# Contrast adjustment: 64 KB rows in three kept buffers, two hardware queues, half-tile DMAs of every second row, and the clip shared between VectorE and ScalarE

## The chip, the cores and the metric

One core of one Trainium2 chip. The metric is device time in microseconds (us) of one execution. The profile adds a "span", from the first to the last instruction it shows, which is about 2 us (1.8 to 2.2 in the profiled runs) shorter than the device time of the same run. Every run of a kernel on one core is called fast unless it was over 1.5% above the fastest run of the same kernel. The first measurement and the three sets of experiments ran at different times, the three sets on three different chips; the kernel before ran beside every set.

## The reference

```python
x = rand(16, 3, 512, 512), float32          # 48 images of 1 MiB, 50.33 MB
mean = np.mean(x, axis=(2, 3), keepdims=True)
out = np.clip(mean + factor * (x - mean), 0, 1)     # factor 1.5
```

Nothing of an image can be written before all of it has been read, because its mean is needed first. So 100.66 MB cross the DMA engines, and each tile goes load, sum, clip, store.

## The kernel before

```python
TILE_IMGS = [4] * 11 + [2, 2]        # 4 MiB tiles of 32 KB rows, two small ones at the end
X_BUFS = 5
...
for i, N in enumerate(TILE_IMGS):
    xt = xpool.tile([P, NMAX * n_pix // P], f32, name="xt")[:, :FREE]
    nc.sync.dma_start(out=xt, in_=src)
    nc.vector.tensor_reduce(out=rsum, in_=xt, axis=X, op=add)          # L77
    nc.tensor.matmul(pbias, blockw[N], rsum, start=True, stop=True)    # L85
    nc.scalar.copy(out=bias, in_=pbias)
    nc.scalar.activation(out=xt, in_=xt, func=Relu, bias=bias, scale=factor)      # L90
    nc.vector.tensor_scalar(out=xt, in0=xt, scalar1=1.0, scalar2=None, op0=min)   # L97
    nc.gpsimd.dma_start(out=dst, in_=xt)                               # L104
```

(The rest sets up the constant matrix that sums over an image's partitions. Cuts are marked by dots.)

Of the kernel before, what the change touches and what calls it, by code (L numbers as in the profile page):

```python
# [1 line left out]

# [4 lines left out]


TILE_IMGS = [4] * 11 + [2, 2]  # L10
X_BUFS = 5
STORE_ENGINE = "gpsimd"


@with_exitstack
def kernel(
    ctx: ExitStack,
    tc: tile.TileContext,
    x: bass.AP,
    factor: float,  # L20
    out: bass.AP,
):
    nc = tc.nc
    P = 128

    B, C, H, W = x.shape
    n_img = B * C
    n_pix = H * W

    factor = float(factor)  # L30
    f32 = mybir.dt.float32

    assert sum(TILE_IMGS) == n_img
    NMAX = max(TILE_IMGS)

    x_f = x.rearrange("b c h w -> (b c h w)")
    out_f = out.rearrange("b c h w -> (b c h w)")

    wconst = (1.0 - factor) / float(n_pix)

    consts = ctx.enter_context(tc.tile_pool(name="consts", bufs=1))
    blockw = {}
    for N in sorted(set(TILE_IMGS)):
        wt = consts.tile([P, P], f32, name=f"blockw{N}")
        PPI = P // N
        if N == 1:
            nc.gpsimd.memset(wt, wconst)
        else:
            nc.gpsimd.memset(wt, 0.0)  # L49
            for b in range(N):  # L50
                nc.gpsimd.memset(wt[b * PPI : (b + 1) * PPI, b * PPI : (b + 1) * PPI], wconst)  # L51
        blockw[N] = wt

    xpool = ctx.enter_context(tc.tile_pool(name="xpool", bufs=X_BUFS))
    rpool = ctx.enter_context(tc.tile_pool(name="rpool", bufs=12))
    bpool = ctx.enter_context(tc.tile_pool(name="bpool", bufs=12))
    psum = ctx.enter_context(tc.tile_pool(name="psum", bufs=8, space=bass.MemoryType.PSUM))

    if STORE_ENGINE == "sync":
        store_eng = nc.sync  # L60
    elif STORE_ENGINE == "act":
        store_eng = nc.scalar
    else:
        store_eng = nc.gpsimd

    pix_off = 0
    for i, N in enumerate(TILE_IMGS):
        FREE = n_pix * N // P
        npix_tile = n_pix * N

        xt = xpool.tile([P, NMAX * n_pix // P], f32, name="xt")[:, :FREE]
        src = bass.AP(tensor=x_f.tensor, offset=pix_off, ap=[[FREE, P], [1, FREE]])
        dst = bass.AP(tensor=out_f.tensor, offset=pix_off, ap=[[FREE, P], [1, FREE]])
        nc.sync.dma_start(out=xt, in_=src)  # L74

        rsum = rpool.tile([P, 1], f32)
        nc.vector.tensor_reduce(  # L77
            out=rsum,
            in_=xt,
            axis=mybir.AxisListType.X,  # L80
            op=mybir.AluOpType.add,
        )

        pbias = psum.tile([P, 1], f32)
        nc.tensor.matmul(pbias, blockw[N], rsum, start=True, stop=True)  # L85

        bias = bpool.tile([P, 1], f32)
        nc.scalar.copy(out=bias, in_=pbias)  # L88

        nc.scalar.activation(  # L90
            out=xt,
            in_=xt,
            func=mybir.ActivationFunctionType.Relu,
            bias=bias,
            scale=factor,
        )
        nc.vector.tensor_scalar(  # L97
            out=xt,
            in0=xt,
            scalar1=1.0,  # L100
            scalar2=None,
            op0=mybir.AluOpType.min,
        )
        store_eng.dma_start(out=dst, in_=xt)  # L104

        pix_off += npix_tile


# [1 line left out]
_INS = ['x', 'factor']  # L110
_OUTS = [((16, 3, 512, 512), 'float32')]
#: Inputs that are plain numbers.
_NUMBERS = {'factor': 1.5}


# [26 lines left out]
```

## Time and profile before

| | kernel before |
|---|---|
| device time, median of 3 | 239.69 us (239.58 to 239.84) |
| span of the profiled run | 238.6 us |
| DMA over the span | 422 GB/s |
| VectorE, ScalarE busy | 66%, 37% |

The page of the kernel before, cut. The row DMA is the busy share of the 16 DMA engines, in tenths, in 40 slices of the span; q1 carries the loads, q0 the stores; the last three lines are groups of instructions with their busy time, the mean ns of one, and the idle time ahead of them with what ended it.

```profile
span 238.6 us, 238 instructions
...
DMA  7999999999999999999999999999999999999995
...
q1 hardware_dynamic: 1872, 50.33, 49.4%
q0 software_dynamic: 1872, 50.33, 49.0%
...
L77 DVE TENSOR_REDUCE rsum<-xt 128x1 f32<-128x8192 f32 (+1 forms) x13 | 104.4, 8029 | 61.7 <-DMA xt<-in_x_dram 61.7
L90 ACT ACTIVATE xt<-xt,bias 128x8192 f32<-128x8192 f32 (+1 forms) x13 | 85.8, 6598 | 0.4
L97 DVE TENSOR_SCALAR xt<-xt 128x8192 f32<-128x8192 f32 (+1 forms) x13 | 53.2, 4091 | 5.0 <-ACT xt L90 5.0
```

The DMA engines are busy throughout and VectorE waits 61.7 us for loads: the kernel is bound by DMA. The stretches view of the same trace gives the rate in the last column; the other columns are each engine's busy time.

```profile
core 0: us, PE busy (x) PEld busy (x) DVE busy (x) ACT busy (x) POOL busy (x), PEclk, DMA share, GB/s
60.00:180.00 120.00, 3.46 (x12) 3.00 (x12) 79.72 (x13) 48.97 (x13) 3.73 (x7) 1.00 1.01 435
210.00:230.00 20.00, 0.56 (x2) 0.50 (x2) 6.71 (x2) 3.87 (x2) 0.53 (x1) 1.00 1.00 432
```

The Trainium skill, "DMA: Bandwidth & Descriptors", section "Where 436 GB/s comes from", gives a ceiling of 435 GB/s; this trace sits on it. The same section says that the HBM side, at about 358 GB/s, binds for transfers between HBM and SBUF; this core ran at 435 GB/s, so that lower limit did not bind here. The timeline of the last small tile:

```profile
211.80 4.42 DVE L77 TENSOR_REDUCE rsum<-xt 128x1 f32<-128x4096 f32 x1 [4.14 <-DMA xt<-in_x_dram]
...
217.16 3.71 ACT L90 ACTIVATE xt<-xt,bias 128x4096 f32<-128x4096 f32 x1
220.90 2.29 DVE L97 TENSOR_SCALAR xt<-xt 128x4096 f32<-128x4096 f32 x1 [4.68 <-ACT xt L90]
223.49 0.53 POOL L104 DMA_DIRECT2D out_dram<-xt  x1 [15.00 <-DVE xt L97]
```

From the last landing (211.80) to the last store's issue (223.49) are 11.7 us.

### The profile page before, as it was taken

How to read it: one execution, taken by the hardware profiler on the slowest of the kernel's cores; microseconds unless marked ns; L12 is line 12 of the kernel's file. 1: busy time of each engine (PE TensorE's matmuls, PEld its weight loads, DVE VectorE, ACT ScalarE, POOL GpSimd, SP SyncE). 2: the span in 40 equal slices, each digit the busy share in tenths (PEclk: the TensorE clock that was granted, in tenths of full speed). 3: DMA queues.
4: the chain of work that ended last, by engine and by line, in shares of the span. 5: the costliest groups of instructions: out<-in, count | busy, mean ns of one | idle time of the engine just before them, and what ended most of it. 6: DMA issues, size and time to landing. Idle time of an engine off the chain costs nothing.

```text
span 238.6 us, 238 instructions
## 1 busy us (share of the span) xinstructions
PE 7.4 (3%) x26; PEld 6.5 (3%) x26; DVE 156.5 (66%) x26; ACT 89.1 (37%) x27; POOL 10.3 (4%) x25
## 2 busy tenths in 40 slices
PE   0000000000000000000000000000000000000000
PEld 0000000000000000000000000000000000000000
DVE  0088999999599079459629909917945979742300
ACT  2002966472906601900920650470190095406000
POOL 2000001000000000000000000000000000500000
DMA  7999999999999999999999999999999999999995
GB/s 269 434 439 439 439 439 352 439 434 439 439 439 439 439 434 434 423 428 412 423 439 439 434 439 439 439 439 439 434 428 426 426 404 428 431 434 439 428 434 214
DMA packets 3744, 100.66 MB, mean 422 GB/s; under 512 B 416, under 2 KB 416, under 8 KB 416
## 3 DMA queue, kind: packets, MB, share of 16 engines
q1 hardware_dynamic: 1872, 50.33, 49.4%
q0 software_dynamic: 1872, 50.33, 49.0%
HBM read 50.33 MB, written 50.33 MB: 422 GB/s over the span
## 4 chain that ended last, share of the span: by engine, by line
issue 38%; DMA 35%; DVE 18%; POOL 2%; POOLq 0%; SPq 0%
DMA xt<-in_x_dram 19%; DMA out_dram<-xt 16%; DVE rsum L77 11%; DVE xt L97 7%; POOL out_dram L104 2%; POOLq L137 0%; SPq L74 0%; POOLq L104 0%
## 5 line engine op out<-in xcount | busy, mean ns | idle before, releaser
L77 DVE TENSOR_REDUCE rsum<-xt 128x1 f32<-128x8192 f32 (+1 forms) x13 | 104.4, 8029 | 61.7 <-DMA xt<-in_x_dram 61.7
L90 ACT ACTIVATE xt<-xt,bias 128x8192 f32<-128x8192 f32 (+1 forms) x13 | 85.8, 6598 | 0.4
L97 DVE TENSOR_SCALAR xt<-xt 128x8192 f32<-128x8192 f32 (+1 forms) x13 | 53.2, 4091 | 5.0 <-ACT xt L90 5.0
L88 ACT COPY bias<-pbias 128x1 f32<-128x1 f32 x13 | 2.1, 160 | 130.6 <-PE pbias L85 130.6
L104 POOL DMA_DIRECT2D out_dram<-xt x13 | 9.0, 692 | 213.0 <-DVE xt L97 212.8
L85 PE MATMUL pbias<-rsum,blockw 128*128 128x1 f32 x26 | 7.4, 355 | 209.5 <-DVE rsum L77 209.5
L85 PEld LDWEIGHTS pbias<-rsum,blockw 128*128 128x128 f32 x26 | 6.5, 311 | 210.3 <-DVE rsum L77 107.1
L88 ACT ACT_TABLE_LOAD x1 | 1.3, 1283 | 0.8 <-PEq L123 0.8
L51 POOL MEMSET blockw<- 32x32 f32 (+1 forms) x6 | 0.8, 128 | 0.2
L49 POOL MEMSET blockw<- 128x128 f32 x2 | 0.3, 205 | 0.3 <-POOLq L123 0.3
L123 POOL MEMSET const-float32-0.0<- 128x1 f32 x1 | 0.1, 104 | 0.2 <-issue 0.2
L123 POOL MEMSET const-bfloat16-1.0<- 128x1 bf16 x1 | 0.1, 113 | 0.0
L123 POOL MEMSET const-uint8-127<- 128x1 uint8 x1 | 0.1, 113 | 0.0
L123 POOL MEMSET const-float32-1.0<- 128x1 f32 x1 | 0.1, 110 | 0.0
## 6 DMA issues: line engine op xcount, KB each, us to landing
xt<-in_x_dram SPq DMA_DIRECT2D x11, 4096.0 KB, 24.6
out_dram<-xt POOLq DMA_DIRECT2D x11, 4096.0 KB, 36.0
xt<-in_x_dram SPq DMA_DIRECT2D x2, 2048.0 KB, 19.5
out_dram<-xt POOLq DMA_DIRECT2D x2, 2048.0 KB, 19.1
```

What stands on the lines that cost most here:

```text
L49: nc.gpsimd.memset(wt, 0.0)
L51: nc.gpsimd.memset(wt[b * PPI : (b + 1) * PPI, b * PPI : (b + 1) * PPI], wconst)
L77: nc.vector.tensor_reduce(out=rsum, in_=xt, axis=mybir.AxisListType.X, op=mybir.AluOpType.add,)
L85: nc.tensor.matmul(pbias, blockw[N], rsum, start=True, stop=True)
L88: nc.scalar.copy(out=bias, in_=pbias)
L90: nc.scalar.activation(out=xt, in_=xt, func=mybir.ActivationFunctionType.Relu, bias=bias, scale=factor,)
L97: nc.vector.tensor_scalar(out=xt, in0=xt, scalar1=1.0, scalar2=None, op0=mybir.AluOpType.min,)
L104: store_eng.dma_start(out=dst, in_=xt)
L123: nc = _bacc.Bacc("TRN2", target_bir_lowering=False, num_devices=1)
```

## The change

The intent is to use larger descriptors, to feed both queues by hardware, and to share the compute so that 8 MB tiles (six of them) still fit under the DMA time. The core of the diff:

```diff
-TILE_IMGS = [4] * 11 + [2, 2]
-X_BUFS = 5
-STORE_ENGINE = "gpsimd"
+ROW = 16384
+BUFS = 3
+HALF = ROW // 2
+OWN = 3840
+CHUNKS = (4096, 4096, 2816, 1536)
+JUNK = 2048
+PARTS = 2
...
+        for r in range(parts):        # parts = 1 for tile 0, else 2
+            nc.sync.dma_start(out=xt[r::parts, :], in_=dram(x_f, t, r, parts))
...
+        nc.vector.tensor_reduce(out=sums[:, 0:1], in_=xt[:, 0:HALF], ...)
+        for j in range(n_act):        # four pieces of 2048 columns
+            nc.scalar.activation(out=junk, in_=xt[:, a : a + JUNK], func=Act.Copy, accum_out=sums[:, 1 + j : 2 + j])
+        for j in range(1 + n_act):
+            nc.tensor.matmul(pbias, blockw, sums[:, j : j + 1], start=j == 0, stop=j == n_act)
         nc.scalar.copy(out=bias, in_=pbias)
+        # own = xt[:, 0:OWN]: VectorE alone, two passes
+        nc.vector.tensor_scalar(out=own, in0=own, scalar1=factor, scalar2=bias, op0=Alu.mult, op1=Alu.add)
+        nc.vector.tensor_scalar(out=own, in0=own, scalar1=0.0, scalar2=1.0, op0=Alu.max, op1=Alu.min)
+        for n in CHUNKS:              # the rest: Relu on ScalarE, min on VectorE
+            ...
+        for r in range(PARTS):
+            nc.scalar.dma_start(out=dram(out_f, t, r, PARTS), in_=xt[r::PARTS, :])
...
+    with tc.manual_schedule():        # three loads, then compute, store and load(t + 3) by turns
```

## The prediction

> **What bounds the kernel now.** The DMA engines. The page has DMA at 9 tenths or more in 38 of 40 slices; VectorE is busy 66%, ScalarE 37%. The stretches view gives 435 GB/s from 60 to 180 us (loads and stores mixed) and 432 from 210 to 230 us (stores alone). The Trainium skill, "DMA: Bandwidth & Descriptors", "Where 436 GB/s comes from", puts the ceiling at 435 GB/s; this trace agrees. All 100.66 MB at 433 GB/s cost 232.5 us. The other 6.1 us of the 238.6 us span: 1.75 us before the first packet, about 0.9 us of slow first packets (1.7 to 2.2 us for 32 KB, later 1.21), 1.8 us after the last packet, under 1 us of skew between engines, about 1 us of dips (419 GB/s from 30 to 60 us, 424 from 180 to 210). VectorE's 61.7 us of waiting for loads (the waits view) is slack.
>
> **What changes.**
> - 32 KB rows become 64 KB rows. Packets of 16 KB took 611 ns, of 32 KB 1213 ns, so one costs about 9 ns beyond its bytes; 96 fewer per engine win at most 0.9 us.
> - Stores leave the GpSimd queue (0.53 us each, one 2.46 us) for ScalarE's hardware queue: perhaps 0.5 us of the dips.
> - Six tiles of 8 MB in three buffers. First landing moves from 13.0 to about 23 us, first store from 36 to about 48 us; loads fill the DMA meanwhile (three buffers take 58 us).
> - Compute per tile (estimates from the trace's durations): VectorE sums half the columns in 8.7 us, ScalarE the other half in four pieces of about 2.0 us; five matmuls about 3 us; bias 0.2; ScalarE's four pieces 3.7+3.7+2.6+1.6 us, VectorE clipping its own 3840 columns meanwhile (2 x 2.2 us); last clip 1 us. About 24 us, against 38.8 us of DMA per tile (16.8 MB at 433 GB/s): hidden.
>
> **The critical path.** Still the DMA, if neither queue runs dry. Each half-tile load waits only for the store of the same rows (checked in the built program's waits). Walking the queues through at 433 GB/s, shared evenly, each refill finds its rows stored 6 us or more before the load queue would run dry. The last load lands near 192 us, its compute ends near 215, and tile 4's store drains near 216. So the last store is ready just when the engines would go idle: a gap of 0 to 2.5 us, the one new cost I expect, growing once compute exceeds about 25 us.
>
> Sum: 238.6 - 0.8 (packets) - 0.5 (queue) + 0.5 (coarser packets at the end) + 0.5 (gap) = 238.3 us span, plus the 1.1 us by which the measured time exceeds the span: about 239.2 us. Range 236.8 to 243.0. Faster by over 2%: 2%; within 2%: 86%; slower: 12%.
>
> **What would show each step.** 60 to 180 us at 434-436 GB/s. First store issued at 46 to 50 us. Tile period near 38.8 us. VectorE waiting for loads from tile 2 on. GpSimd idle after the memsets. DMA share dipping only near 215 us. Reduce to store 23 to 26 us.
>
> **What would make it wrong.** Chiefly the DMAs of every second row. The skill, "SBUF — State Buffer", "Door 1: The DMA port swizzle", has ports serving fixed partition groups; every second row still reaches all 16, but 4 rows per engine may put two engines on one port at once. No trace here shows 64-row DMAs. If they clash, the stretches of loads alone (24 to 46 us) and stores alone (last 35 us) fall well below 430 GB/s and the time rises by 5 to 30 us. Second: compute over 25 us. Third: arbitration favouring one queue, moving the last landing.

## The result, and the profile after

The changed kernel took 240.68 us (median of 4: 240.44, 240.46, 240.89 and one slow run of 245.28), the kernel before 239.66 us beside it. The ratio is 1.0038, with a 95% interval of 1.0022 to 1.0054: the same at 2%, about 0.9 us slower (the interval excludes 1). Ratios here are the mean time of one kernel's fast runs over the mean of the other's fast runs of the same rounds, so not quite the ratio of the medians. A large rebuild bought nothing.

The page of the changed kernel, cut (q10 are the stores now):

```profile
span 238.4 us, 354 instructions
...
DMA  9898989899899998989898989899998989898894
...
q1 hardware_dynamic: 944, 50.33, 49.5%
q10 hardware_dynamic: 960, 50.33, 48.8%
...
L85 DVE TENSOR_REDUCE sums<-x 128x1 f32<-128x8192 f32 x6 | 52.1, 8685 | 74.6 <-DMA x<-in_x_dram 59.6
L91 ACT ACTIVATE junk<-x 128x2048 f32<-128x2048 f32 x24 | 45.8, 1910 | 79.6 <-DMA x<-in_x_dram 76.7
L109 ACT ACTIVATE x<-x,bias 128x4096 f32<-128x4096 f32 (+2 forms) x24 | 67.8, 2897 | 0.2
...
L96 PE MATMUL pbias<-sums,blockw 128*128 128x1 f32 x60 | 13.7, 354 | 190.1 <-DVE sums L85 190.1
```

Half as many packets move the same bytes, and VectorE and ScalarE share the work at 50% each. Both still wait for loads (59.6 and 76.7 us). The page's rates swing now, because a packet of 64 KB takes 2.42 us and is counted whole, so short stretches are rough: the stretches view gives 430 GB/s from 60 to 180 us, while packets of 2.418 us for 65536 bytes on 16 engines make 434 GB/s.

The end of the changed kernel's timeline, the last tile:

```profile
192.76 8.69 DVE L85 TENSOR_REDUCE sums<-x 128x1 f32<-128x8192 f32 x1 [14.98 <-issue]
...
201.50 2.29 PE L96 MATMUL pbias<-sums,blockw 128*128 128x1 f32 x10 [36.32 <-DVE sums L85]
...
204.02 11.31 ACT L109 ACTIVATE x<-x,bias 128x4096 f32<-128x4096 f32 x4
...
213.89 2.50 DVE L110 TENSOR_SCALAR x<-x 128x2816 f32<-128x2816 f32 x2 [0.24 <-ACT x L109]
216.42 1.13 ACTq L116 DMA_DIRECT2D out_dram<-x  x2
```

From the last landing (192.7) to the store's issue (216.42) are 23.7 us, twice what it was. The stretches view around that issue shows what the DMA engines did meanwhile:

```profile
core 0: us, PE busy (x) PEld busy (x) DVE busy (x) ACT busy (x) POOL busy (x), PEclk, DMA share, GB/s
...
216.40:217.50 1.10, 0.00 (x0) 0.00 (x0) 0.00 (x0) 0.00 (x0) 0.00 (x0) 1.00 0.00 0
217.50:227.20 9.70, 0.00 (x0) 0.00 (x0) 0.00 (x0) 0.00 (x0) 0.00 (x0) 1.00 1.00 432
```

They had nothing to do: the store of the tile before had drained and the last was not ready. The first packet of the last store started at 217.56 us.

The trace records each packet's queue, size, start and duration. Chaining packets that follow each other sorts them onto the 16 engines (the records do not name the engine), and gives an account of the span, in us per engine (before: a second trace of the kernel before, from experiment c_before, since the first trace is from a run about 1 us slower than the usual one; see below; it ran at another time than the changed kernel):

```
                                            before   after
until the first packet                        1.74    1.74
packets at their usual duration             233.04  232.13   (176 x 1.213 + 32 x 0.611; 96 x 2.418)
slow packets at the very start                0.68    0.54
slow load packets as the stores begin         0.65    1.22
slow packets later                            0.01    0.12
idle, less overlap of packets                -0.17    1.37
last packet ends at                         235.95  237.12
from there to the end of the span             1.67    1.24
span                                        237.62  238.36
```

The row of idle time is what is left over, and holds the stagger of the engines too; the pauses after 205 us alone are 0.02 us before and 1.21 us after, at the median engine.

So the larger packets won 0.91 us, about as forecast. A dead time near the end, about 1.2 us at the median engine, and a worse start of the stores (+0.57 us) took it back.

The larger packets have a part in that dead time. A load is reported as landed by a small record of 4 bytes on each engine. While loads ran alone, the last of these records came as the data ended (both at 22.35 us for the first tile). With stores running beside it, the last load's record came later by the length of one store packet: 2.41 us in the changed kernel (data ended at 189.90 us, record at 192.31 us), 1.21 us with the 32 KB rows of c_before (208.07 and 209.28 us). It was 2.41 us in all nine traces with 64 KB stores that were looked at, and 1.2 us in all three with 32 KB stores. So, as an estimate from these two numbers, the last tile's compute began 1.2 us later than it would have with 32 KB stores beside it. That is as much as the dead time. No run changes this wait alone, so its share of the dead time is not shown.

### The profile page after: what moved, and what is told of

Read it like the earlier page. It is cut to its first block, busy times and chain, and to the rows that moved or that the text cites. A ratio compares the mean times of both kernels' runs of the same rounds, so it can differ in the third digit from the quotient of the medians.

```text
span 238.4 us, 354 instructions
## 1 busy us (share of the span) xinstructions
PE 13.7 (6%) x60; PEld 13.2 (6%) x60; DVE 120.3 (50%) x42; ACT 118.1 (50%) x79; POOL 1.4 (1%) x17
## 4 chain that ended last, share of the span: by engine, by line
DMA 34%; DVE 18%; ACT 17%; another core or an unknown queue 10%; issue 7%; PE 4%; DVEq 0%; SPq 0%
DMA out_dram<-x 20%; ACT x L109 16%; DVE sums L85 15%; DMA x<-in_x_dram 14%; PE pbias L96 4%; DVE x L110 4%; DVEq L156 0%; ACT bias L98 0%; SPq L79 0%; DVEq L85 0%
## 5 line engine op out<-in xcount | busy, mean ns | idle before, releaser
L85 DVE TENSOR_REDUCE sums<-x 128x1 f32<-128x8192 f32 x6 | 52.1, 8685 | 74.6 <-DMA x<-in_x_dram 59.6
L91 ACT ACTIVATE junk<-x 128x2048 f32<-128x2048 f32 x24 | 45.8, 1910 | 79.6 <-DMA x<-in_x_dram 76.7
L109 ACT ACTIVATE x<-x,bias 128x4096 f32<-128x4096 f32 (+2 forms) x24 | 67.8, 2897 | 0.2
L110 DVE TENSOR_SCALAR x<-x 128x4096 f32<-128x4096 f32 (+2 forms) x24 | 42.5, 1790 | 5.8 <-ACT x L109 5.8
L96 PE MATMUL pbias<-sums,blockw 128*128 128x1 f32 x60 | 13.7, 354 | 190.1 <-DVE sums L85 190.1
L96 PEld LDWEIGHTS pbias<-sums,blockw 128*128 128x128 f32 x60 | 13.2, 329 | 190.5 <-DVE sums L85 158.9
L100 DVE TENSOR_SCALAR x<-x,bias 128x3840 f32<-128x3840 f32 x6 | 13.3, 2221 | 15.5 <-ACT bias L98 15.5
L103 DVE TENSOR_SCALAR x<-x 128x3840 f32<-128x3840 f32 x6 | 13.0, 2159 | 0.2
L98 ACT COPY bias<-pbias 128x1 f32<-128x1 f32 x6 | 1.0, 160 | 16.6 <-PE pbias L96 16.6
L91 ACT ACTIVATION_READ_ACCUMULATOR junk<-x 128x1 f32 x24 | 4.5, 186 | 0.0
```

The costliest lines, as they stand in the source:

```text
L85: nc.vector.tensor_reduce(out=sums[:, 0:1], in_=xt[:, 0:HALF], axis=mybir.AxisListType.X, op=Alu.add)
L91: nc.scalar.activation(out=junk, in_=xt[:, a : a + JUNK], func=Act.Copy, accum_out=sums[:, 1 + j : 2 + j])
L96: nc.tensor.matmul(pbias, blockw, sums[:, j : j + 1], start=j == 0, stop=j == n_act)
L100: nc.vector.tensor_scalar(out=own, in0=own, scalar1=factor, scalar2=bias, op0=Alu.mult, op1=Alu.add)
L103: nc.vector.tensor_scalar(out=own, in0=own, scalar1=0.0, scalar2=1.0, op0=Alu.max, op1=Alu.min)
L109: nc.scalar.activation(out=part, in_=part, func=Act.Relu, bias=bias, scale=factor)
```

## The experiments

My theory after the result was that the dead time before the last store costs about 1.2 us. Rivals were that the stores' new queue costs time outside the span, and that five matmuls a tile do. A second theory came up on the way: that single slow load packets cost more with this kernel. Twelve kernels ran, in three sets; all gave correct results.

### One matmul instead of five, in all tiles, and in the last alone

```diff
-        for j in range(1 + n_act):
-            nc.tensor.matmul(pbias, blockw, sums[:, j : j + 1], start=j == 0, stop=j == n_act)
+        tot = rpool.tile([P, 1], f32, name="tot")         # e2: only where t == n_tiles - 1
+        nc.vector.tensor_reduce(out=tot, in_=sums, axis=X, op=Alu.add)
+        nc.tensor.matmul(pbias, blockw, tot, start=True, stop=True)
```

> The changed kernel with one matmul per tile instead of five (VectorE adds the five partial sums first), in every tile: about 1.6 us less compute per tile. My theory: the last gap (1.2 us of idle DMA engines before the last store) is set by the DMA queues as much as by the compute. Stores that start 1.6 us earlier take bandwidth from the loads earlier, so the last load lands about 1.6 us later and its compute ends where it did, near 216 us; the time stays within 0.3 us of the changed kernel (240.2 to 240.8 us). Rival, compute simply lies on the path at the end: 1.2 us less, about 239.3 us. Second question, the time outside the span: if the number of instructions (354 in the changed kernel, 238 before) makes the measured time exceed the span by 2.1 us instead of 1.1, then the excess falls here, to about 1.5 us, as 96 matmul and weight-load instructions go; if not, it stays at 2.1 us.

> The same, but in the last tile alone. Both theories of the gap: everything up to the last landing is as in the changed kernel, the last store is issued 1.6 us earlier, near 214.8 us, before tile 4's store has drained (216.9 us), so the gap closes and the time falls by 1.0 to 1.2 us, to about 239.3 us (span about 237.2 us). Together with the run that does it in every tile this tells whether the gap belongs to the last tile's compute alone. If the time does not fall, the gap was not what it looked like.

Measured: 243.50 us (241.62 to 246.3) and 242.08 us (241.37 to 244.88), against 240.38 us for the kernel before in the same set. Neither prediction held, and neither decides between the theories, because something else showed up that swamps 1.2 us. In e1's trace, which is of a slow run (245.77 us), the matmuls did shrink from 2.29 to 0.58 us, but one of the 16 engines lost 6.0 us to slow packets after 60 us (4.2 us of it in loads), a single engine lost 5.0 us in e2 (a fast run), and the last load landed at 199.3 and 198.1 us instead of 192.7. Fifteen engines of e1 had finished their loads by 189.9 us, the last one at 196.5 us. The whole tile waits for that engine. The engines in step then idled 6.3 us at the median before the last store; the late one did not idle at all, since its own backlog lasted as long.

Whether fewer matmuls in every tile would move the last landing, as I argued, stays open. On the question of time outside the span, e1's device time exceeded its span by 1.8 us and e2's by 2.1 us.

### Stores from GpSimd in the changed kernel; stores from ScalarE in the kernel before

```diff
-            nc.scalar.dma_start(out=dram(out_f, t, r, PARTS), in_=xt[r::PARTS, :])    # e3
+            nc.gpsimd.dma_start(out=dram(out_f, t, r, PARTS), in_=xt[r::PARTS, :])
-STORE_ENGINE = "gpsimd"                                                               # e4
+STORE_ENGINE = "act"
```

> The changed kernel with its stores issued from GpSimd as before, nothing else. If the second hardware queue is what makes the measured time exceed the span by 2.1 us (1.1 us in the kernel before), the excess falls to about 1.1 us and the time to about 239.7 us. If the excess comes from something else it stays at 2.1 us. The stretch in which the stores begin should dip by about 1.2 us in sum either way, as both kernels show such a dip with different queues; if the hardware queue shortened it, it grows here.

> The kernel before with its stores issued from ScalarE's hardware queue, nothing else. If the queue makes the excess over the span, it rises from 1.1 to 2.1 us here and the time to about 240.6 us with an unchanged span of 238.6 us. If not, the time stays within 0.3 us of 239.7 us.

Measured: e3 243.92 us (243.48 to 248.88), with 2.1 us over its span of 242.0 us. e4 272.01 us, with 1.9 us over its span. The kernel before itself had 1.9 to 2.1 us over its span in all 11 runs of this set. So the excess of 2 us belongs to every kernel here, and the rival falls. My "1.1 us" had set the median time of three runs against the span of a profiled run that must have been a slower one: in these sets, runs of the kernel before with a span of 238.6 us took 240.5 to 240.6 us.

e3's start of the stores cost 1.01 us per engine in slow packets (1.16 and 1.30 in e1 and e2 on the same chip), so the hardware queue is not what shortens it. e3's fast runs took 1.0159 times the kernel before (1.0120 to 1.0199), more than e1 and e2 (1.0098 and 1.0082); the changed kernel itself did not run in this set, so what the GpSimd queue costs here is not shown.

e4 missed by 32 us, and I had not foreseen it. On ScalarE's instruction stream a store waits for VectorE's clip, and whatever the scheduler put behind it waits too:

```profile
ACT bias L88 <- PE pbias L85: 101.3, 6, 29.1
DVE rsum L77 <- DMA xt<-in_x_dram: 88.1, 9, 20.3
ACT bias L88 <- DVE xt L97: 60.7, 4, 23.1
```

This is e4's waits view (who waited for what, us in total, times, longest). The third line is new: ScalarE stood 60.7 us waiting for VectorE's clip, on behalf of stores, and the packet records show the median DMA engine idle for 28 us. The changed kernel has its order written by hand, with each tile's stores as the last thing that ScalarE does for that tile; that this is why it escapes was not tested.

### Controls on one chip: the changed kernel and the kernel before

No edit (copies of both kernels).

> The changed kernel itself again, as a control: the first four experiments ran on another chip or in another condition than the first measurement, and there one DMA engine in each trace lost 4 to 6 us to load packets of 2.7 to 3.5 us instead of 2.42. If that belongs to the chip and not to those edits, the changed kernel takes 241 to 244 us here too, with one engine late by several us at the last landing. If it belongs to the edits, it takes 240.5 us with all engines within 1 us of each other, as in its first trace.

> The kernel before again, for its trace beside the changed kernel's on one chip. If slow load packets are the chip's doing, they are here too: one engine late by some us, and a spread of some us between the engines' last packets, with the time at 240.4 us (it ran 239.7 to 241.35 us in the last set). If they come only with 64 KB rows, the load packets after 60 us are all 1.21 us here and the engines end within 1.2 us of each other.

Measured: the changed kernel 242.63 us (240.50 to 244.18), the kernel before 239.67 us (239.56 to 240.06). So slow load packets come without my edits too, though no engine of c_after lost the 5 to 6 us seen on one engine in e1 and e2. In c_after's trace three engines lost 0.9 to 1.2 us each to slow packets after 60 us, and the last store came at 218.25 us instead of 216.42, with 2.9 us of idle time at the median engine. In c_before's trace not one packet after 42 us was slow by over 0.05 us, and all engines ended within 0.4 us of each other.

One caution: the kernel before also ran 11 times as the baseline of this set, where it took 239.58 to 241.69 us. Its times are not always as tight as in the six runs of c_before, and I have no trace of the slower ones.

### The last tile stored in column pieces

```diff
+        if t == n_tiles - 1: piece(t, 0, OWN)      # piece: nc.sync.dma_start of all 128 rows, columns c to c + n
         for n in CHUNKS:
             ...
+            if t == n_tiles - 1: piece(t, c, n)
...
-            store(t)
+            if t < n_tiles - 1: store(t)
```

> The changed kernel, but the last tile is stored in five column pieces from the SP queue (idle by then), each as soon as it is clipped: the first piece about 8 us earlier than the two row halves. My theory: the last gap closes (1.2 us where all engines are in step; more for the engines that are in step where one lags), so the time falls by about 1.1 us against the changed kernel if the engines are in step. If one engine lags by 5 us or more, it has no gap of its own in the changed kernel (its backlog lasts until the last store), and the time falls by less than 0.5 us. Rival, the gap is not what sets the time: no change in either case.

Measured: 241.39 us (240.66 to 242.38), beside 242.63 us for the changed kernel on the same chip. The mean of the fast runs fell by 0.6 us (242.13 to 241.52), but the ratios to the kernel before, 1.0057 (1.0032 to 1.0081) and 1.0080 (1.0029 to 1.0130), overlap, so the times alone do not decide. The trace does: the idle time before the last store went from 2.9 us at the median engine to 0.0. Thirteen engines ended by 236.1 us, where they ended at 238.9 us in c_after. The other three, with 1.1 to 1.3 us of slow packets after 60 us where the rest had none, ended at 237.4 to 237.9 us and set the time. So the gap is real and can be closed, and behind it stands a lag of single engines. The stretch in which c_after's DMA engines had nothing to do (first line) is at work in this run (second line):

```profile
216.40:217.50 1.10, 0.00 (x0) 0.00 (x0) 1.10 (x2) 0.76 (x1) 0.00 (x0) 1.00 0.01 0
216.40:217.50 1.10, 0.00 (x0) 0.00 (x0) 1.10 (x2) 0.98 (x1) 0.00 (x0) 1.00 0.86 367
```

### Half-size tiles

```diff
-ROW = 16384
-BUFS = 3
+ROW = 8192
+BUFS = 6
-OWN = 3840
-CHUNKS = (4096, 4096, 2816, 1536)
+OWN = 1920
+CHUNKS = (2048, 2048, 1408, 768)
```

> The changed kernel with 32 KB rows: twelve tiles of 4 MB in six buffers, all else scaled by half (own columns 1920, clip pieces 2048, 2048, 1408, 768). Compute of a tile falls from 23.7 to about 13 us, so the last store is ready well before the stores drain: no gap, which is worth 1.2 us; packets of 32 KB cost 0.5 us more over the run (433.2 instead of 434.1 GB/s). Expected 0.7 us under the changed kernel, about the kernel before. If the 64 KB rows are what makes single load packets slow, these vanish here and the time falls by more, 2 us or so under the changed kernel on this chip.

Measured: 239.72 us (239.59 to 240.27), level with the kernel before (ratio 0.9984, interval 0.9966 to 1.0003) and 2.3 us under the changed kernel on that chip (means of the fast runs, 239.79 and 242.13 us). Landing to last issue is 12.9 us (209.24 to 222.09), no engine idles more than 0.2 us at a time, and the load packets after 60 us were slow by only 0.3 us over all 16 engines (3.1 us in c_after). Two hardware queues, half-tile DMAs and the shared clip are all still there, so none of these alone is at fault. Row size, tile size and the number of buffers changed together here; this run does not separate them.

### A longer last tile

```diff
+        if t == n_tiles - 1:        # one more clip pass over 8192 columns, no effect on the result
+            nc.vector.tensor_scalar(out=xt[:, 0:HALF], in0=xt[:, 0:HALF], scalar1=0.0, scalar2=1.0, op0=Alu.max, op1=Alu.min)
```

> The changed kernel with one more clip pass over half the columns of the last tile (VectorE, about 4.4 us, no effect on the result). If the last tile's compute is on the critical path, the time rises by the whole 4.4 us, to 245 to 248 us (the changed kernel took 240.4 to 244.2 us on two chips), and the idle stretch of the DMA engines before the last store grows by 4.4 us. If there were slack, as I first thought there almost was, it rises by less than 2 us.

Measured: 246.33 us (245.82 to 249.9). Its trace has the last landing at 194.0 us, the last store's issue at 222.03 us, 28.0 us later instead of 23.7, and a median idle time of 6.7 us. Its stretches view, with the share of the DMA engines next to last:

```profile
216.00:219.00 3.00, 0.00 (x0) 0.00 (x0) 3.00 (x3) 0.59 (x1) 0.00 (x0) 1.00 0.00 0
219.00:223.00 4.00, 0.00 (x0) 0.00 (x0) 2.99 (x1) 0.00 (x0) 0.00 (x0) 1.00 0.00 0
223.00:242.60 19.60, 0.00 (x0) 0.00 (x0) 0.00 (x0) 0.00 (x0) 0.00 (x0) 1.00 0.99 428
```

Against c_after on another chip (landing 194.6 us, idle 2.9 us, last packet 238.9 us; here the last packet ended at 242.7 us), which began its last tile only 0.6 us later, the added 4.3 us of compute became 3.8 us of idle and 3.8 us of later last packet. The last tile's compute is on the critical path nearly one for one; there is no slack.

### Whole-tile DMAs

```diff
-PARTS = 2
+PARTS = 1
```

> The changed kernel with whole-tile DMAs (128 rows, one load and one store a tile). A load then waits for the whole store of its buffer's last tile. Walking the queues through with the measured rates (434 GB/s, stores ready 23.7 us after a landing, 3.2 us from the end of a store to the next load's first packet) gives the last landing at 202 us instead of 192 us, its store ready at 226 us while tile 4's store still drains at 217 us, so about 9.5 us of idle DMA engines and a time near 250 us. If halves do not matter, as stores fill the DMA while the loads wait, the time stays at 240.5 to 244 us.

Measured: 248.75 us (247.95 to 249.89). The last landing came at 201.2 us, the last store was issued at 224.9 us, and the median engine idled 9.6 us, all within 1.3 us of what was walked through:

```profile
200.00:216.00 16.00, 2.29 (x10) 2.21 (x10) 12.15 (x3) 11.67 (x10) 0.00 (x0) 1.00 0.92 397
218.00:225.50 7.50, 0.00 (x0) 0.00 (x0) 5.90 (x4) 5.80 (x3) 0.00 (x0) 1.00 0.00 0
225.50:245.00 19.50, 0.00 (x0) 0.00 (x0) 0.00 (x0) 0.00 (x0) 0.00 (x0) 1.00 1.00 430
```

In its middle the DMA engines were never idle: while a load waited for its buffer, the stores took the engines. The loss comes at the end, where stores that ran early are missing. The halves are what lets this kernel live with three buffers.

### Halves of neighbouring rows

```diff
-            nc.sync.dma_start(out=xt[r::parts, :], ...)
+            nc.sync.dma_start(out=xt[r * (P // parts) : (r + 1) * (P // parts), :], ...)    # stores alike
```

> The changed kernel with its two DMAs a tile moving rows 0 to 63 and rows 64 to 127 instead of every second row. If 64 neighbouring partitions reach only half the ports, as the Trainium skill says, loads alone (24 to 46 us) and stores alone (the last 40 us) run near 217 GB/s instead of 434, and the time rises by 20 to 50 us. If the 16 engines are the limit whatever the rows, the rate stays at 434 GB/s and the time at 240.5 to 244 us.

Measured: 363.07 us (359.96 to 368.54); the profiled run was the slowest of the four. Its stretches view shows loads of whole tiles alone, loads of halves alone, both queues, and stores of halves alone:

```profile
4.00:21.00 17.00, 0.00 (x0) 0.00 (x0) 0.00 (x0) 0.00 (x0) 0.00 (x0) 1.00 1.00 432
24.00:44.00 20.00, 2.26 (x10) 2.21 (x10) 16.61 (x5) 16.85 (x12) 0.00 (x0) 1.00 1.01 210
60.00:300.00 240.00, 9.17 (x40) 8.83 (x40) 80.36 (x29) 78.09 (x53) 0.00 (x0) 1.00 0.98 304
330.00:360.00 30.00, 0.00 (x0) 0.00 (x0) 0.00 (x0) 0.00 (x0) 0.00 (x0) 1.00 0.93 194
```

Half the rate, with the engines "busy" all along: only their packets got longer. The Trainium skill, "SBUF — State Buffer", section "Door 1: The DMA port swizzle", says that partitions 0 to 63 reach 8 of 16 ports; 210 GB/s agrees. I had put the cost at 20 to 50 us, as I took mixed loads and stores to be spared; they ran at 304 GB/s, and it was 120 us. Every second row, in contrast, ran at full rate: in the changed kernel's first trace the packets of its half loads between 24 and 40 us took the same 2.42 us as those of whole tiles.

### Only the last tile halved

```diff
+    JOBS = [(t * full, ROW, t % BUFS, 0) for t in range(n_tiles - 1)]       # offset, row, buffer, first column
+    JOBS += [(last + h * full // 2, ROW // 2, (n_tiles - 1) % BUFS, h * ROW // 2) for h in range(2)]
```

(with compute, loads and stores taking row length, buffer and columns from the job, and a second summing matrix for 32 KB rows)

> The changed kernel with its last tile cut into two tiles of 32 KB rows (four images each) in the two halves of the same buffer; the five others keep 64 KB rows. Compute after the last landing falls from 23.7 to about 13 us, so the last store is ready before the stores drain: no gap. In step, the last packet then ends near 236.0 us instead of 237.1 and the time is 239.4 us, level with the kernel before (239.6 us) or 0.2 us under. With a lagging engine, its lag stays: 240 to 242 us. If the time does not fall below the changed kernel's, the gap was not worth what I say.

Measured: 243.89 us (241.33 to 246.02, two of the four runs slow; the fast two took 241.33 and 241.87 us), ratio 1.0068 (1.0041 to 1.0094) to the kernel before. It does not beat that kernel; against the changed kernel, whose ratios were 1.0038 and 1.0080 on other chips, the times do not decide. The last compute shortened to 12.9 us (214.57 to 227.42), but the last landing moved from 192.7 to 214.6 us, and the median engine still idled 2.4 us. The page's queue lines for the stretch from 155 to 205 us, in which 32 KB loads ran beside 64 KB stores, say why (packets, MB, share of the engines' time):

```profile
q10 hardware_dynamic: 270, 13.76, 63.7%
q1 hardware_dynamic: 281, 7.64, 35.8%
```

Without the small records of 4 bytes these are 210 store packets and 233 load packets. The queues got nearly the same number of packets, so the loads, with packets half as long, got about a third of the bandwidth. On the chained engines 314 of the 427 steps from one packet to the next changed the queue, so the two were served mostly by turns, a packet each, whatever their size. The Trainium skill, "DMA: Bandwidth & Descriptors", section "Queues, rings and completion order", says so (round-robin "at *packet* granularity"); here a whole row of 32 or 64 KB counted as the packet. The last load's record again came 2.41 us after its data, the length of a 64 KB store packet, though the load's own packets were of 32 KB.

## Why the prediction was right or wrong

- **Bound by DMA, time within 2%: right.** 240.68 us lies inside 236.8 to 243.0 us, and 1.5 us above the 239.2 us named. The sign was missed: 239.2 us is 0.5 us under the kernel before, and the time rose by 0.9 us.
- **Packets, -0.8 us: right.** Usual packet time per engine fell from 233.04 to 232.13 us. (112 packets fewer per engine, 208 to 96, and not the 96 fewer that the prediction counts.)
- **Compute hidden, about 24 us a tile: right.** Reduce to store took 23.7 us, the first store was issued at 46.45 us, and the last three tiles landed 38.65 us apart. The last tile's compute, with no load left beside it, is the exception: see the gap below.
- **Stores on the hardware queue, -0.5 us in the dips: wrong.** Slow load packets as the stores begin rose from 0.65 to 1.22 us per engine. It is about one packet per engine, slow by up to 1.39 us at 64 KB, and one or two, slow by up to 0.67 us, at 32 KB (c_before); putting the stores back on GpSimd left 1.01 us. At the end of the span, though, less time passed after the last packet: 1.2 to 1.4 us with ScalarE's queue, but for e1 with 1.6 us, against 1.65 to 1.81 us in the three traces with GpSimd's.
- **Coarser packets at the end, +0.5 us: absent.** All engines ended within 0.2 us of each other. What coarser packets did cost is the later record of each landing, 1.2 us, which the prediction does not have.
- **The gap, +0.5 us of 0 to 2.5: right in kind, too small.** It was 1.2 us at the median engine in the first trace, 2.9 us on the chip of the controls. That e7's added 4.3 us became 3.8 us of idle time, and that column pieces brought the idle time to zero, shows it.
- **Device time 1.1 us over the span: wrong, about 2 us (1.8 to 2.2 in the profiled runs) in every kernel.** The span I started from was 1 us too long for the median run, which cancels this. That the forecast span of 238.3 us met the measured 238.4 us is therefore luck: the change of the span was forecast as -0.3 us and measured as +0.7 us (237.6 to 238.4). The sum as written also gives 239.4 us and not 239.2.
- **"Each refill finds its rows stored 6 us or more before the load queue would run dry": wrong for the first.** The load queue stopped at 71.95 us and resumed at 76.1 us, as the data of store 0's first half ended at 69.1 us but its last record came at 71.50 us, and the first packet 4.6 us after that. It cost no DMA time: stores filled in.
- **Clash of every-second-row DMAs: did not happen.** It is neighbouring rows that clash.
- **Not foreseen: the spread.** The changed kernel ran 240.4 to 245.3 us. The likely reason is that the last tile waits for the slowest of 16 engines and has no slack behind it, as in the traces of e1, e2 and c_after; its own slow runs left no trace. Slow load packets went with the 64 KB kernels in most traces (16-engine sums after 60 us between 0.3 and 10.3 us) and were nearly absent with the two 32 KB kernels on the same chip (0.0 and 0.3 us). But e4, with 32 KB rows on another chip, had 20.1 us of them, its stores stopping and starting again. Why a load packet is slow at all, and whether 64 KB rows cause it, is open.

Where the expected gain went: 0.9 us were won per engine in the packets, and given back at both ends of the store stream, in the gap (with the later record of the last landing) and in the start.

## What to carry to other kernels

In a kernel that streams through at the DMA ceiling, the last tile decides: its landing-to-store time must be shorter than the store backlog behind which it hides, on the slowest DMA engine and not on the mean one, so large tiles in few buffers need a small last step. Larger packets save little time each, and on the queue beside they delay the report of a landing by a whole packet (2.41 instead of 1.21 us here). Give both queues packets of one size, because turns are mostly by packet (e10). When a tile must be moved in parts, take every second row and not neighbouring halves, and put a store into a compute engine's stream only where nothing behind it is urgent.

## What the Trainium skill lacked or had wrong

- "DMA: Bandwidth & Descriptors", "Rules for kernel authors", advises against splitting a transfer into partition halves. That leaves out that halves of every second row ran at full rate (2.42 us a packet, as for whole tiles) and freed buffers sooner: the changed kernel took 1.0038 and 1.0080 times the kernel before, its whole-tile form 1.0369 times.
- The same page, "SWDGE vs HWDGE vs iDMA", calls a packet at most 4096 B by preference. In these traces a row of 32 KB (1.213 us) or 64 KB (2.418 us) is one record, and in e10 the two queues mostly alternated by such records: 233 against 210, and 7.64 against 13.76 MB.
- No page that I read has the slow load packets when the first stores begin (0.65 to 0.72 us per engine with 32 KB rows, 0.95 us in e4, 1.0 to 1.4 us with 64 KB). For engines that lag, the same page has only that engines 7 and 15 are usually slower ("Latency and other measured facts"), with a guess that holds for GpSimd's queue alone; in e1 and e2, with both queues fed by hardware, single engines lost 6.0 and 5.0 us. The records do not name the engine.
- No page gives the wait of a load's last record behind a store packet: 1.21 us with 32 KB stores, 2.41 us with 64 KB stores.
- "SBUF — State Buffer", "Door 1: The DMA port swizzle", was right about half the ports (210 GB/s), but does not say what mixed loads and stores do then: 304 GB/s.
